# 24 warming matmuls where 14 stood, and a later place on ScalarE for the decay factors of group 0

## The chip, the cores and the metric

One core of a Trainium2 chip runs the whole program. The metric is device microseconds of one execution; the time of a kernel is the median of its runs. Five engines work beside each other, each in its own order: TensorE (PE, with its weight loads PEld), VectorE (DVE), ScalarE (ACT), GpSimd (POOL) and SyncE (SP), which issues most transfers.

## The reference

A decoder block on 256 tokens of 1024 channels, all in float32. The normalized input goes through one wide projection. Its columns feed a state-space mixer (8 groups of 4 heads, a causal convolution, a scan in chunks of 128 tokens), an attention of 16 heads, and gates. Both branches are projected, merged, projected once more and added to the input; a gated feed-forward part with a convolution and a last norm follow.

```python
hn = rmsnorm(x, norm1_w)
proj = hn @ w_in
z, xbc_raw, dt_raw, q, k, v, g_raw = jnp.split(proj, IN_OFFSETS, axis=-1)
y_ssd = ssd_mixer(z, xbc_raw, dt_raw, ssd_conv_w, ssd_conv_b, ssd_dt_bias, ssd_a_log, ssd_d, ssd_norm_w)
...
y_att = moba_attention(q, k, v.reshape(b, s, ATT_N_HEADS, ATT_HEAD_DIM))
...
merged = g_ssd * (y_ssd @ w_ssd_proj) + g_att * (y_att @ w_att_proj)
x = x + merged @ w_out
h2 = rmsnorm(x, norm2_w)
a, gb = jnp.split(h2 @ w_ffn_up, 2, axis=-1)
a = causal_dwconv(a, ffn_conv_w, ffn_conv_b)
return x + (jax.nn.silu(a) * gb) @ w_ffn_down
```

In the mixer the decay between two tokens of a chunk is an exponential of a difference of running sums, and it is multiplied by the product of C and B:

```python
L = jnp.exp(segsum(Adt))
CB = jnp.einsum('bclgn,bcsgn->bcgls', Cc, Bc)
y_diag = jnp.einsum('bcgls,bgrcls,bcsgrp->bclgrp', CB, L, Xc)
```

## The kernel before

The weights come in tiles of 1 MB, in the order of the list `seq`. Each tile (a unit here) is loaded into one of three `raw` buffers, and `split_unit` (L86) divides it in two halves. ScalarE casts each half to `hi` (L95), VectorE subtracts to get `lo` (L96). Four buffers of each hold two units. Activations are kept as such pairs too, so that a float32 product becomes three fast matmuls: hi by hi, hi by the lo of the other, lo by hi (L152 to L154 for a unit, 48 matmuls; L181 to L183 for the gates; L348 to L350 for v). `next_unit` returns unit i, issues loads up to i + 2 and writes the splits up to unit i + 1.

The head: `xtok` is loaded and its squares are summed; VectorE makes two diagonal matrices `dg` of the norm's factors (L266). Ahead of this TensorE multiplies a tile of ones by itself WARM times (L73), into a PSUM tile that nothing reads. Sixteen transposes (L271, eight for each half of the tokens) write x times `dg` into four PSUM tiles `xps`, two channel blocks in each. From these ScalarE casts the eight `hn` (L235), and VectorE makes their lo parts (L237). Then unit 0 can start on TensorE (`u_bc(0)`).

A group g of the mixer has the units bc, x, qk and then v, z or gate tiles. In group 0 the units are 0 bc, 1 x, 2 qk, 3 z, 4 and 5 the gates; group 1 has 6 bc, 7 x, 8 qk, 9 v, 10 z. The running sums of the decay go out to DRAM (`acsT_d`) and come back spread over all partitions (`acsB`), both by GpSimd's queue. `s_cb(g)` makes the product `pcb` on TensorE and its masked copy `cb` on VectorE; then ScalarE turns `acsB` into the decay factors `mx` with 13 activations (L376 to L379), and VectorE multiplies them by `cb` (L381). `s_y(g)` uses them in the product `py` (L403), which TensorE does behind unit x of the next group; the scores `s_ps` (L432) follow.

What sets the order: the tile scheduler orders the instructions of each engine by the program's order, priorities and its own estimate of times. TensorE has the program's order, once the head is over. `tc.issue_after(i)` keeps the instructions inside it behind instruction i on the engine; in `s_cb` they stand behind the tanh of z (`z_tanh`), in the last group behind the copy of q and k. Waits between engines are added by what is read and written.

Of the kernel before, what the change touches and what calls it, by code (L numbers as in the profile page):

```python
# [11 lines left out]
AF = mybir.ActivationFunctionType  # L12
# [10 lines left out]
NG = 8  # L23
# [10 lines left out]
C_DTB, C_AL = 304, 336  # L34
NPAR = 368

WARM = 14


def block_kernel(tc, xtok_d, par_d, nf_d, con_d, rope_d, wdt_d, win_d, wgate_d, bg_d, watt_d, wssd_d, wout_d, wup_d, wdn_d, out_d):  # L40
    nc = tc.nc
    st = ExitStack()
    pool = lambda name, bufs=1, **kw: st.enter_context(tc.tile_pool(name=name, bufs=bufs, **kw))
    with st:
# [26 lines left out]
        with tc.manual_schedule(engines=PE_ONLY):  # L71
            for _ in range(WARM):
                nc.tensor.matmul(warm[:, 0, 0:P], ones, ones, start=True, stop=True)  # L73
# [14 lines left out]
        def split_unit(raw, nk=KD):  # L88

            halves = []  # L90
            for k0 in range(0, nk, 4):
                n = min(4, nk - k0)
                hi = wpool.tile([P, 4, 256], F32R, tag="hi", bufs=4, name="hi")
                lo = wpool.tile([P, 4, 256], F32R, tag="lo", bufs=4, name="lo")
                nc.scalar.activation(hi[:, :n], raw[:, k0 : k0 + n], AF.Copy)  # L95
                split_unit.last = nc.vector.tensor_tensor(lo[:, :n], raw[:, k0 : k0 + n], hi[:, :n].bitcast(F32),  # L96
                                                          op=ALU.subtract)
                halves.append((hi, lo, n))
            return halves
# [21 lines left out]
        def next_unit():  # L121

            i = next_unit.i
            next_unit.i += 1
            load_to(i + 3)
            while len(units) < min(i + 2, len(seq)):
                n = len(units)
                units.append(split_unit(raws[n], seq[n][1]))
            return units[i]
# [3 lines left out]
        def mm_unit(ps, halves, act, first=True, last=True, k0=0, apart=False):  # L133


            tiles = [(hi, lo, kk) for hi, lo, n in halves for kk in range(n)]
            nk = len(tiles)
            km = [(k, m) for k in range(nk) for m in range(2)]
            if apart:
                km.sort(key=lambda x: x[1])  # L140
                ps = [p[:, 0, :] for p in ps]
            else:
                ps = [ps[:, m, :] for m in range(2)]
            with tc.manual_schedule(engines=PE_ONLY):
                for k, m in km:
                    hi, lo, kk = tiles[k]
                    xh, xl = act[k0 + k][:, 0, :], act[k0 + k][:, 1, :]
                    wh = hi[:, kk, m * P : m * P + P]
                    wl = lo[:, kk, m * P : m * P + P]
                    a = first and k == 0 and (m == 0 or apart)  # L150
                    z = last and k == nk - 1 and (m == 1 or apart)
                    nc.tensor.matmul(ps[m], wh, xh, start=a, stop=False)  # L152
                    nc.tensor.matmul(ps[m], wh, xl, start=False, stop=False)  # L153
                    nc.tensor.matmul(ps[m], wl, xh, start=False, stop=z)  # L154
# [30 lines left out]
        def mm_tile():  # L185
            return ps_mm.tile([P, 2, T], F32, tag="mm", bufs=3, name="mm")
# [108 lines left out]
        S = [dict() for _ in range(NG)]  # L295
# [4 lines left out]
        def u_bc(g):  # L300
            hv = next_unit()
            ps = mm_tile()
            mm_unit(ps, hv, hn)
            bc = S[g]["bc"] = ssp.tile([P, 2, T], F32, tag="bc", bufs=1, name="bc")
            conv_silu(bc, ps, (16 + g, 24 + g))

        def u_x(g):
            hv = next_unit()
            ps = mm_tile()
            mm_unit(ps, hv, hn)  # L310
            xs = S[g]["xs"] = ssp.tile([P, 2, T], F32, tag="xs", bufs=2, name="xs")
            conv_silu(xs, ps, (2 * g, 2 * g + 1))
# [50 lines left out]
        def s_cb(g):  # L363
            bc = S[g]["bc"]
            pcb = ps_s.tile([P, 4, P], F32, tag="ss", bufs=2, name="pcb")
            nc.tensor.matmul(flat(pcb[:, 0:2]), bc[:, 0, 0:P], bc[:, 1, :], start=True, stop=True)
            nc.tensor.matmul(pcb[:, 2], bc[:, 0, P:T], bc[:, 1, P:T], start=True, stop=True)
            cb = ssp.tile([P, 3, P], F32, tag="cb", bufs=1, name="cb")
            nc.vector.tensor_tensor(cb, pcb[:, 0:3], mmask, op=ALU.mult)
            acsB = S[g]["acsB"]  # L370
            mx = S[g]["mx"] = ssp.tile([P, 4, 3, P], F32, tag="mx", bufs=1, name="mx")
            with tc.issue_after(S[g]["qk_copy" if g == NG - 1 else "z_tanh"].ins):
                for r in range(4):
                    h = 4 * g + r
                    for c, b in ((0, 0), (1, 2)):
                        nc.scalar.activation(mx[:, r, b], acsB[:, r, c * P : c * P + P], AF.Relu, scale=-1.0,  # L376
                                             bias=acs[:, c, h : h + 1])
                    nc.scalar.activation(mx[:, r, 1], acsB[:, r, P:T], AF.Exp, bias=alm[:, h : h + 1])
                nc.scalar.activation(mx[:, :, 0:3:2], mx[:, :, 0:3:2], AF.Exp, scale=-1.0)  # L379
            m2 = mx.rearrange("p h b l -> p h (b l)")  # L380
            nc.vector.tensor_tensor(m2, m2, flat(cb)[:, None, :].to_broadcast([P, 4, 3 * P]), op=ALU.mult)  # L381

        def s_xt(g):
            xs = S[g]["xs"]
            pxt = ps_s.tile([P, 2, T], F32, tag="ss", bufs=2, name="pxt")
            for c in range(2):
                for m in range(2):
                    nc.tensor.transpose(pxt[:, c, m * P : m * P + P], xs[:, m, c * P : c * P + P], ident)
            xt = S[g]["xt"] = ssp.tile([P, 2, 4, 64], F32, tag="xt", bufs=1, name="xt")
            nc.vector.tensor_tensor(xt, pxt.rearrange("p c (h d) -> p c h d", h=4),  # L390
                                    dt[:, :, 4 * g : 4 * g + 4][:, :, :, None].to_broadcast([P, 2, 4, 64]), op=ALU.mult)
# [20 lines left out]
        def s_st(g):  # L412
            S[g]["ry"] = rms_stat([S[g]["sqy"][:, 0]], 1.0 / 256)
# [36 lines left out]
        def a_t(g):  # L450
            S[g]["pt"] = []
            for j in range(2):
                pt_ps = ps_s.tile([P, 4, P], F32, tag="at", bufs=2, name="pt_ps")
                for b in range(3):
                    nc.tensor.transpose(pt_ps[:, b], S[g]["pr"][j][:, b], ident)  # L455
                pt = atp.tile([P, 3, P], F32, tag="pt", bufs=2, name="pt")
                nc.scalar.activation(pt, pt_ps[:, 0:3], AF.Copy)
                S[g]["pt"].append(pt)
# [112 lines left out]
        def small_1(g):  # L571
            if 0 <= g - 1 < NG:
                s_y(g - 1)
                a_s(g - 1)
            if 0 <= g - 2:
                a_o(g - 2)
                if g < NG:
                    s_pb(g - 2)

        def small_2(g):  # L580
            if g < NG:
                s_cb(g)
                s_xt(g)
            if 0 <= g - 1:
                s_st(g - 1)
                a_t(g - 1)
            if g == NG:
                s_pb(g - 2)

        for g in range(NG):  # L590
            if g:
                u_bc(g)
                u_x(g)
                small_1(g)
                load_acs(g)
            u_qk(g)
            if g == 0:
                for c in range(2):
                    tc.keep_in_program_order(nc.gpsimd.dma_start(gates[:, c], bg_d.partition_broadcast(P)))
                u_z(g)  # L600
                turn_qk(g)
                dt_sums()
                gate = u_gate(0)
                next(gate)
                dt_turn()
                load_acs(0)
                next(gate)
                next(gate)
                small_2(g)
                next(gate)  # L610
            elif g == NG - 1:
                u_z(g)
                turn_qk(g)
                small_2(g)
                u_v(g)
            elif g % 2:
                u_v(g)
                turn_qk(g)
                u_z(g)
                small_2(g)  # L620
            else:
                u_z(g)
                turn_qk(g)
                gate = u_gate(g // 2)
                next(gate)
                next(gate)
                small_2(g)
                next(gate)
                next(gate)
# [187 lines left out]
        for h in range(2):  # L817
# [3 lines left out]
            hv, k0 = next_unit(), DOWN[-1][0]  # L821
# [125 lines left out]
```

## Time and profile before

| | us |
|---|---|
| median of 3 runs | 604.04 |
| lowest and highest run | 602.41, 607.84 |
| the profiled execution | 604.41 |
| its span, first to last instruction | 602.6 |

The profile is of one execution. A row of a timeline gives the start in us from the span's start, the duration in us (of several merged instructions together, with their number as x), engine, line, operation and tiles, and in brackets how long the engine was idle ahead of it and what ended that. A TensorE matmul lasts longer than the step to the next one, since they are pipelined. The granted clock is TensorE's, 1.00 being 2.4 GHz and 0.50 being 1.2 GHz.

### The profile page before, as it was taken

The page shows a single profiled execution, that of the slowest core. Times are in us where ns is not written, and L with a number is a line of the kernel's source. Part 1 is how long each engine was busy: PE and PEld are TensorE (multiplying, and loading weights), DVE is VectorE, ACT ScalarE, POOL GpSimd, SP SyncE. Part 2 cuts the span into 40 slices and gives each one's busy share as a digit, 9 for nine tenths or more (in the row PEclk, how much of TensorE's full clock was granted, in tenths as well). Part 3 has the DMA queues.
Part 4 walks back from the last instruction along what each step waited for, and adds up shares of the span by engine and source line. Part 5 has one row for each costly group of instructions (what it writes and reads, how often), then busy time and mean ns, then how long its engine had stood idle before and what let it go on. Part 6 is the DMA issues. An engine that isn't in the chain of part 4 may idle for free.

```text
span 602.6 us, 10067 instructions
## 1 busy us (share of the span) xinstructions
PE 589.6 (98%) x3886; PEld 528.6 (88%) x3886; DVE 459.8 (76%) x889; ACT 372.5 (62%) x675; POOL 17.9 (3%) x35
## 2 busy tenths in 40 slices
PE   7999999999999999999999999999999999999994
PEld 7899899999999999999998888889888888888883
DVE  3894989879798797978988446667888888884643
ACT  4654686866769567695686334456766666665432
POOL 0010000000000000010000000000000000000100
PEclk8999999999999999999999999999999999999997
DMA  8665646353363544645334855645456455464602
GB/s 314 238 230 239 234 156 212 136 218 140 145 232 139 193 141 148 241 145 176 140 129 157 291 187 185 206 152 201 154 197 204 155 200 205 123 228 150 239 34 70
DMA packets 17728, 109.73 MB, mean 182 GB/s; under 512 B 2177, under 2 KB 2561, under 8 KB 5649
## 3 DMA queue, kind: packets, MB, share of 16 engines
q1 hardware_dynamic: 15264, 100.42, 47.3%
q0 software_dynamic: 1984, 6.85, 3.1%
q10 hardware_dynamic: 432, 1.84, 0.8%
q8 instruction: 30, 0.49, 0.3%
q14 instruction: 18, 0.14, 0.1%
HBM read 107.49 MB, written 1.08 MB: 180 GB/s over the span
## 4 chain that ended last, share of the span: by engine, by line
PE 94%; DMA 3%; ACT 1%; issue 1%; DVE 1%; SPq 0%; ACTq 0%; DVEq 0%
PE up L164 12%; PE mm L152 10%; PE mm L154 10%; PE mm L153 10%; PE mm L181 10%; PE mm L182 10%; PE mm L183 10%; PE up L165 6%; PE py L403 2%; PE mm L348 1%; PE mm L350 1%; PE mm L349 1%; PE s_ps L432 1%; PE po L469 1%; DMA xtok<-in_xtok_dram 1%; PE pt_ps L455 1%
## 5 line engine op out<-in xcount | busy, mean ns | idle before, releaser
L96 DVE TENSOR_TENSOR lo<-raw,hi 128x1024 fp32r<-128x1024 f32 x186 | 227.1, 1226 | 83.6 <-ACT hi L95 82.8
L95 ACT ACTIVATE hi<-raw 128x1024 fp32r<-128x1024 f32 x186 | 195.0, 1056 | 142.1 <-PE mm L183 65.4
L152 PE MATMUL mm<-hn,hi 128*128 128x256 f32 x512 | 146.0, 285 | 0.4 <-ACT hi L95 0.4
L154 PE MATMUL mm<-hn,lo 128*128 128x256 f32 x512 | 144.9, 283 | 0.8 <-DVE lo L96 0.8
L153 PE MATMUL mm<-hn,hi 128*128 128x256 f32 x512 | 145.0, 283 | 0.4 <-DVE hn L237 0.4
L164 PE MATMUL up<-xw,hi 128*128 128x512 f32 x320 | 113.1, 399 | 0.0
L152 PEld LDWEIGHTS mm<-hn,hi 128*128 128x128 f32 x512 | 98.1, 192 | 1.5 <-ACT hi L95 0.9
L154 PEld LDWEIGHTS mm<-hn,lo 128*128 128x128 f32 x512 | 98.2, 192 | 1.0 <-DVE lo L96 1.0
L153 PEld LDWEIGHTS mm<-hn,hi 128*128 128x128 f32 x512 | 98.2, 192 | 0.9 <-DVE hn L237 0.8
L165 PE MATMUL up<-xw,lo 128*128 128x256 f32 x320 | 89.9, 281 | 0.0
L164 PEld LDWEIGHTS up<-xw,hi 128*128 128x128 f32 x320 | 60.1, 188 | 15.0
L165 PEld LDWEIGHTS up<-xw,lo 128*128 128x128 f32 x320 | 60.5, 189 | 0.0
L289 DVE SCALAR_TENSOR_TENSOR cacc<-mm,par,cacc 128x255 f32<-128x255 f32 (+2 forms) x96 | 44.5, 477 | 2.2 <-ACT cacc L285 1.4
L181 PE MATMUL mm<-hi,act 128*128 128x512 f32 (+1 forms) x92 | 34.9, 380 | 0.0
L182 PE MATMUL mm<-lo,act 128*128 128x512 f32 (+1 forms) x92 | 34.9, 380 | 0.0
L183 PE MATMUL mm<-hi,act 128*128 128x512 f32 (+1 forms) x92 | 34.9, 380 | 0.0
L181 PE MATMUL mm<-hi,hn 128*128 128x512 f32 x64 | 25.5, 398 | 0.0
L181 PE MATMUL mm<-hi,yn 128*128 128x512 f32 x64 | 25.2, 394 | 0.0
L376 ACT ACTIVATE mx<-acsB,acs 128x128 f32<-128x128 f32 x64 | 21.9, 391 | 5.1 <-DMA acsB<-acsT_d 5.1
L182 PE MATMUL mm<-lo,hn 128*128 128x512 f32 x64 | 25.0, 390 | 0.0
L183 PE MATMUL mm<-hi,hn 128*128 128x512 f32 x64 | 25.0, 390 | 0.0
L182 PE MATMUL mm<-lo,yn 128*128 128x512 f32 x64 | 24.9, 390 | 0.0
(196 smaller groups left out, 970.6 us busy)
## 6 DMA issues: line engine op xcount, KB each, us to landing
raw<-in_win_dram SPq DMA_DIRECT2D x35, 1024.0 KB, 4.8
raw<-in_wup_dram SPq DMA_DIRECT2D x22, 1024.0 KB, 4.8
raw<-in_wdn_dram SPq DMA_DIRECT2D x10, 1024.0 KB, 4.9
raw<-in_wgate_dram SPq DMA_DIRECT2D x8, 1024.0 KB, 5.0
raw<-in_wssd_dram SPq DMA_DIRECT2D x8, 1024.0 KB, 4.8
acsB<-acsT_d POOLq DMA_DIRECT2D x8, 512.0 KB, 4.5
raw<-in_watt_dram SPq DMA_DIRECT2D x4, 1024.0 KB, 5.0
raw<-in_wout_dram SPq DMA_DIRECT2D x4, 1024.0 KB, 5.1
```

What stands on the lines that cost most here:

```text
L95: nc.scalar.activation(hi[:, :n], raw[:, k0 : k0 + n], AF.Copy)
L96: split_unit.last = nc.vector.tensor_tensor(lo[:, :n], raw[:, k0 : k0 + n], hi[:, :n].bitcast(F32), op=ALU.subtract)
L152: nc.tensor.matmul(ps[m], wh, xh, start=a, stop=False)
L153: nc.tensor.matmul(ps[m], wh, xl, start=False, stop=False)
L154: nc.tensor.matmul(ps[m], wl, xh, start=False, stop=z)
L164: nc.tensor.matmul(ps[:, m].rearrange("p a b -> p (a b)"), wh, both, start=(k == 0), stop=False)
L165: nc.tensor.matmul(ps[:, m, 1], wl, act[k][:, 0, :], start=False, stop=(k == len(tiles) - 1))
L181: nc.tensor.matmul(o, xh, wh, start=(k == 0 if apart else k0 + k == 0), stop=False)
L182: nc.tensor.matmul(o, xh, wl, start=False, stop=False)
L183: nc.tensor.matmul(o, xl, wh, start=False, stop=(k0 + k == nk - 1))
L289: nc.vector.scalar_tensor_tensor(acc[:, s:], src[:, m, : T - s], w(m, 3 - s), acc[:, s:], op0=ALU.mult, op1=ALU.add)
L376: nc.scalar.activation(mx[:, r, b], acsB[:, r, c * P : c * P + P], AF.Relu, scale=-1.0, bias=acs[:, c, h : h + 1])
```

## The change

`WARM` is 24, not 14. `s_cb` is cut in two: `s_mx` is the part that makes `mx` and multiplies it, and takes the instruction behind which it stands. For groups 1 to 7 it is called where it stood, behind the same instruction. For group 0 it is called inside group 1, after `u_bc(1)`, behind the last hi split that has been written there, which is that of unit 7's second half.

```diff
--- before.py
+++ after.py
@@ -34,7 +34,7 @@
 C_DTB, C_AL = 304, 336
 NPAR = 368
 
-WARM = 14
+WARM = 24
 
 
 def block_kernel(tc, xtok_d, par_d, nf_d, con_d, rope_d, wdt_d, win_d, wgate_d, bg_d, watt_d, wssd_d, wout_d, wup_d, wdn_d, out_d):
@@ -92,7 +92,7 @@
                 n = min(4, nk - k0)
                 hi = wpool.tile([P, 4, 256], F32R, tag="hi", bufs=4, name="hi")
                 lo = wpool.tile([P, 4, 256], F32R, tag="lo", bufs=4, name="lo")
-                nc.scalar.activation(hi[:, :n], raw[:, k0 : k0 + n], AF.Copy)
+                split_unit.last_hi = nc.scalar.activation(hi[:, :n], raw[:, k0 : k0 + n], AF.Copy)
                 split_unit.last = nc.vector.tensor_tensor(lo[:, :n], raw[:, k0 : k0 + n], hi[:, :n].bitcast(F32),
                                                           op=ALU.subtract)
                 halves.append((hi, lo, n))
@@ -367,9 +367,12 @@
             nc.tensor.matmul(pcb[:, 2], bc[:, 0, P:T], bc[:, 1, P:T], start=True, stop=True)
             cb = ssp.tile([P, 3, P], F32, tag="cb", bufs=1, name="cb")
             nc.vector.tensor_tensor(cb, pcb[:, 0:3], mmask, op=ALU.mult)
-            acsB = S[g]["acsB"]
+            S[g]["cb"] = cb
+
+        def s_mx(g, behind):
+            acsB, cb = S[g]["acsB"], S[g]["cb"]
             mx = S[g]["mx"] = ssp.tile([P, 4, 3, P], F32, tag="mx", bufs=1, name="mx")
-            with tc.issue_after(S[g]["qk_copy" if g == NG - 1 else "z_tanh"].ins):
+            with tc.issue_after(behind.ins):
                 for r in range(4):
                     h = 4 * g + r
                     for c, b in ((0, 0), (1, 2)):
@@ -580,6 +583,8 @@
         def small_2(g):
             if g < NG:
                 s_cb(g)
+                if g:
+                    s_mx(g, S[g]["qk_copy" if g == NG - 1 else "z_tanh"])
                 s_xt(g)
             if 0 <= g - 1:
                 s_st(g - 1)
@@ -590,6 +595,8 @@
         for g in range(NG):
             if g:
                 u_bc(g)
+                if g == 1:
+                    s_mx(0, split_unit.last_hi)
                 u_x(g)
                 small_1(g)
                 load_acs(g)
```

TensorE at the very start, after the change: `warm` are the warming matmuls, `xps` the transposes, and the last two rows begin unit 0.

```order
L73 MATMUL warm<-ones 128x128 x21
L271 MATMUL xps<-dg,xtok 128x128 x7
L73 MATMUL warm<-ones 128x128
L271 MATMUL xps<-dg,xtok 128x128 x2
L73 MATMUL warm<-ones 128x128
L271 MATMUL xps<-dg,xtok 128x128
L73 MATMUL warm<-ones 128x128
L271 MATMUL xps<-dg,xtok 128x128 x6
L152 MATMUL mm<-hn,hi 128x256
L153 MATMUL mm<-hn,hi 128x256
```

Before, 14 warming matmuls stood there in a row and 16 transposes behind them; of the ten more, three now stand among the transposes.

ScalarE in the head, before the change: `hi` are the two halves of unit 0 and then of unit 1, `hn` the eight casts, `cacc` the convolution of unit 0.

```order
L95 ACTIVATE hi<-raw 128x1024
L235 ACTIVATE hn<-xps,par 128x256 x2
L95 ACTIVATE hi<-raw 128x1024
L235 ACTIVATE hn<-xps,par 128x256 x6
L95 ACTIVATE hi<-raw 128x1024 x2
L285 ACTIVATE cacc<-mm,par 128x256 x2
```

Here the second half's split stands between the second and the third cast.

And the same stretch of ScalarE after the change:

```order
L518 ACTIVATE nega<-par 128x32
L95 ACTIVATE hi<-raw 128x1024 x2
L235 ACTIVATE hn<-xps,par 128x256 x8
L95 ACTIVATE hi<-raw 128x1024 x2
L285 ACTIVATE cacc<-mm,par 128x256 x2
```

It moved ahead of all of them; on VectorE `lo` and the lo parts of `hn` moved alike.

ScalarE behind the decay factors of group 0, before the change: the first row is the last of their 13 activations, `gates` are the two gate tanhs, and the three `hi` are units 7b, 8a and 8b.

```order
L379 ACTIVATE mx<-mx 128x4x2x128
L566 ACTIVATE gates<-gates 128x512 x2
L95 ACTIVATE hi<-raw 128x1024 x3
L285 ACTIVATE cacc<-mm,par 128x256 x2
L95 ACTIVATE hi<-raw 128x1024
L292 ACTIVATE th<-cacc 128x256
```

After it the gate tanhs and the split of 7b stand ahead of the 13, and this follows them:

```order
L382 ACTIVATE mx<-mx 128x4x2x128
L285 ACTIVATE cacc<-mm,par 128x256 x2
L95 ACTIVATE hi<-raw 128x1024 x4
L292 ACTIVATE th<-cacc 128x256
L285 ACTIVATE cacc<-mm,par 128x256 x2
L292 ACTIVATE th<-cacc 128x256 x2
```

The four splits are units 8 and 9; the last of them moved ahead of the first tanh of unit 6's convolution.

VectorE in group 1, after the change, from the attention's maxima (ISA) to the split of unit 9's second half, the one `lo` here:

```order
L293 SCALAR_TENSOR_TENSOR xs<-th,cacc 128x256
L413 TENSOR_TENSOR zt<-zt 128x256
L444 TENSOR_SCALAR sm<-sm 128x2
L442 ISA pr,sm<-s_ps,con 128x128
L442 ISA sm 128x1
L442 ISA pr,sm<-s_ps,con 128x256
L442 ISA sm 128x1
L96 TENSOR_TENSOR lo<-raw,hi 128x1024
```

Before, this split stood earlier, between the last convolution step of unit 6 and the product `bc`, ahead of all of unit 7's convolution; behind the maxima came unit 10's.

## Rows read from the trace of the kernel before

**Rows 1.** The page's first part: busy time, share of the span, instructions.

```profile
PE 589.6 (98%) x3886; PEld 528.6 (88%) x3886; DVE 459.8 (76%) x889; ACT 372.5 (62%) x675; POOL 17.9 (3%) x35
```

**Rows 2.** TensorE's waits: us in total, times, longest.

```profile
PE xps L271 <- DVE dg L266: 2.2, 1, 2.2
PE warm L73 <- DVE ones L66: 1.1, 1, 1.1
PE mm L154 <- DVE lo L96: 0.8, 1, 0.8
PE mm L153 <- DVE hn L237: 0.4, 1, 0.4
PE mm L152 <- ACT hi L95: 0.4, 1, 0.4
```

**Rows 3.** TensorE's timeline in the head: start, duration, instructions, idle before.

```profile
1.05 5.64 PE L73 MATMUL warm<-ones 128*128 128x128 f32 x28 [1.05 <-DVE ones L66]
8.88 5.47 PE L271 MATMUL xps<-dg,xtok 128*128 128x128 f32 x32 [2.18 <-DVE dg L266]
...
16.54 0.38 PE L153 MATMUL mm<-hn,hi 128*128 128x256 f32 x1 [0.39 <-DVE hn L237]
...
20.71 0.28 PE L154 MATMUL mm<-hn,lo 128*128 128x256 f32 x1
```

**Rows 4.** TensorE's timeline in three short windows, x the records in each.

```profile
5.70 1.00 PE L73 MATMUL warm<-ones 128*128 128x128 f32 x7
...
10.67 1.70 PE L271 MATMUL xps<-dg,xtok 128*128 128x128 f32 x7
...
12.73 1.50 PE L271 MATMUL xps<-dg,xtok 128*128 128x128 f32 x12
```

**Rows 5.** Two windows: busy by engine, then granted clock, DMA share, GB/s.

```profile
10.00:11.00 1.00, 1.00 (x7) 1.00 (x6) 0.87 (x3) 0.51 (x1) 0.00 (x0) 0.50 1.04 389
13.00:14.00 1.00, 1.00 (x12) 1.00 (x11) 0.08 (x1) 0.95 (x3) 0.00 (x0) 1.00 0.99 418
```

**Rows 6.** ScalarE's timeline at the decay factors of group 0.

```profile
56.10 0.76 ACT L376 ACTIVATE mx<-acsB,acs 128x128 f32<-128x128 f32 x2 [5.09 <-DMA acsB<-acsT_d]
...
61.68 2.94 ACT L95 ACTIVATE hi<-raw 128x1024 fp32r<-128x1024 f32 x3
```

**Rows 7.** TensorE's timeline around unit 7b, the product and the scores.

```profile
62.11 0.28 PE L154 MATMUL mm<-hn,lo 128*128 128x256 f32 x1
...
66.86 1.52 PE L403 MATMUL py<-mx,xt 128*64 128x256 f32 x16
...
69.16 0.39 PE L152 MATMUL mm<-hn,hi 128*128 128x256 f32 x1
```

**Rows 8.** ScalarE's timeline in the head: the first two casts.

```profile
13.04 0.84 ACT L235 ACTIVATE hn<-xps,par 128x256 fp32r<-128x256 f32 x2 [2.54 <-PE xps L271]
```

**Rows 9.** The first weight tile's two loads: issue, and time to landing.

```profile
L85 SPq DMA_DIRECT2D raw<-in_win_dram x2: 432/432/432, 3.0 to 3.5; - x2
...
DMA to landing us min/median/max: 6.4/6.8/7.2
```

**Rows 10.** VectorE's timeline in the head.

```profile
10.54 1.23 DVE L96 TENSOR_TENSOR lo<-raw,hi 128x1024 fp32r<-128x1024 f32 x1
...
16.00 2.44 DVE L237 SCALAR_TENSOR_TENSOR hn<-xps,par,hn 128x256 fp32r<-128x256 f32 x6
```

**Rows 11.** VectorE's timeline from group 0 into group 1.

```profile
60.77 1.76 DVE L381 TENSOR_TENSOR mx<-mx,cb 128x1536 f32<-128x1536 f32 x1 [6.28 <-ACT mx L379]
62.76 3.50 DVE L96 TENSOR_TENSOR lo<-raw,hi 128x1024 fp32r<-128x1024 f32 x3 [0.23 <-ACT hi L95]
...
71.83 0.48 DVE L289 SCALAR_TENSOR_TENSOR cacc<-mm,par,cacc 128x255 f32<-128x255 f32 x1
72.23 0.47 DVE L407 SCALAR_TENSOR_TENSOR yg<-xs,par,py 128x256 f32<-128x256 f32 x1
...
77.74 1.22 DVE L96 TENSOR_TENSOR lo<-raw,hi 128x1024 fp32r<-128x1024 f32 x1
```
## The prediction

> **What bounds the kernel now.** I read the busy table first: TensorE is busy for 98% of the span [rows 1]. The reader is to see that another engine matters only where it makes TensorE wait. The list of TensorE's waits comes next [rows 2]. It has five entries, 4.8 us together, in a span of 602.6 us: 2.2 us ahead of the input transposes `xps` (for `dg`), 1.1 us for the first memset, and three smaller ones (0.8, 0.4, 0.4 us) in the projections. The change can win back only these, or work that TensorE does at half clock. So two stretches were read closely, 0 to 21 us and 50 to 78 us. I call unit n the n-th weight tile of `seq` (group 0 is units 0 to 5, group 1 begins with 6), and a and b its halves.
>
> In the head, 14 warming matmuls (28 records, two a matmul) run from 1.05 to 6.69 us, TensorE then idles for 2.2 us, and the 16 transposes (32 records) run from 8.88 to 14.35 us [rows 3]. The step from record to record tells the clock. Seven xps records from 10.67 us take 1.70 us; less the last one's own 0.42 us that is 1.28 / 6 = 0.213 us a step. Twelve from 12.73 us take 1.50 us, so (1.50 - 0.28) / 11 = 0.111 us [rows 4]. The granted clock beside them is 0.50 (1.2 GHz) and 1.00 (2.4 GHz) [rows 5]. The last seven warm records already went at (1.00 - 0.28) / 6 = 0.12 us [rows 4]: the clock had risen before 6 us, fell after the idle 2.2 us, and rose again within the transposes. All 32 at the fast step would take 31 x 0.111 + 0.28 = 3.7 us; they took 5.47, so (5.47 - 3.7) / 0.102 = 17 of them were slow. Then unit 0 starts, stops, and goes on at 16.54 us; its last matmul is at 20.71 us [rows 3].
>
> In the second stretch ScalarE stands still for 5.09 us in front of `mx` until `acsB` lands, and the hi split of unit 7b, queued behind it, starts only at 61.68 us [rows 6]. TensorE wants that half just after 62.11 us, and the product `py` that follows unit 7 starts at 66.86 us [rows 7].
>
> **The warm matmuls.** The new order puts 21 in front of the transposes and 3 among them. The seven more in front are 14 records. At the step of 0.12 us of the last warm ones they end at 6.69 + 14 x 0.12 = 8.4 us, ahead of `dg` (xps started at 8.88 us), so they delay nothing. At 0.213 us they would end at 9.7 us and delay by 0.8 us, the other end. I take the first: the same matmuls were fast by then. TensorE then idles 0.5 us, not 2.2. No row shows how the clock takes a gap of 0.5 us; 2.2 us behind some 1 us of fast work made it fall. I take it to stay at 2.4 GHz, because TensorE would have worked nearly all the time since the rise. The three inner ones cost 6 x 0.111 = 0.7 us. Then 32 + 6 = 38 records end at 8.88 + 37 x 0.111 + 0.28 = 13.3 us, not 14.35. The first PSUM tile is full after 24 records, at 8.88 + 23 x 0.111 + 0.28 = 11.7 us, where before ScalarE took it at 13.04 us [rows 8].
>
> **What the order of the splits does with it.** ScalarE now does both hi splits of unit 0 ahead of all eight `hn` casts, VectorE both lo splits ahead of all eight `hn` differences. Weight half 0b was issued at 3.5 us and landed 7.2 us later, at 10.7 us [rows 9]. So hi 0b (2.94 / 3 = 0.98 us a split [rows 6]) ends near 11.7 us, when the PSUM tile for the first `hn` is full anyway. VectorE's first lo ends at 10.54 + 1.23 = 11.77 us, the second at 13.0 us, and the differences follow at 2.44 / 6 = 0.41 us each [rows 10]: the first is done at 13.4 us, and each next one before TensorE, which stays on one `hn` for 6 x 0.12 = 0.72 us, asks for it. The second matmul of unit 0 thus starts at 13.4 us and the 48th 46 x 0.12 = 5.5 us later, at 19.0 us with a slow first record, where 20.71 us stood [rows 3]. **Term 1: 1.7 us gained.** With no wait for VectorE at all it would be 13.3 + 47 x 0.12 = 18.9 us, 1.8 us gained; the lower ends stand with the rivals. The next units don't hold it: TensorE waits for nothing else up to 62 us [rows 2], their splits follow its release of buffers, and the fourth load, which waits for lo 0b, goes out sooner.
>
> **The decay factors of group 0.** The 13 activations are the same; only their place moves, behind hi 7b and the two gate tanhs. They issue no transfer; the next `acsB` load on GpSimd's queue waits for them as it did. So hi 7b no longer stands behind the wait for `acsB`. Its buffer comes free when TensorE ends the gate unit, 72 matmuls x 0.12 = 8.6 us ahead of 62.2 us, near 53.6 us; hi and lo (0.98 and 1.23 us) are done by 56 us, over 6 us early (all in the times of before, from which term 1 goes off). Without the wait unit 7b takes 24 x 0.12 = 2.9 us from 62.23 us, and `py` starts at 65.2 us with 0.1 us for the new shape, where 66.86 us stood [rows 7]. **Term 2: 1.65 us gained.** That is more than the two named waits (0.4 and 0.8 us), since each restart has slow first records too.
>
> What is late next? On ScalarE the conv scalings of unit 6, the hi splits of units 8 and 9 and the conv tanhs now stand behind `mx`, which ends no later than before, since `acsB` sets its start. VectorE's product of `mx` still ends at 60.77 + 1.76 = 62.5 us [rows 11], 2.7 us before `py`. The tight place is lo 9b: VectorE's order now has it behind the softmax maxima. From 62.5 us on come three lo splits at 3.50 / 3 = 1.15 us and six conv and `bc` steps at 0.40 us (71.83 to 72.23), up to 68.3 us. Then come the operations that took 5.91 us from 71.83 to 77.74 us [rows 11], and two more at 0.40 us, so lo 9b runs from 75.0 to 76.3 us. TensorE asks for it at 65.2 + 2.3 (py and scores, 66.86 to 69.16 us [rows 7]) + 48 x 0.12 (unit 8) + 25 x 0.12 = 76.3 us. It just fits; I charge 0.05 us, and 1.0 us as the bound for an error in that chain.
>
> **Sum.** 1.7 + 1.65 - 0.05 = 3.3 us. The profiled execution took 604.41 us, so 601.1 us. It stands 0.37 us above the median of 604.04 us, so it is a usual run. Some 20 us later the orders of all engines are the same again, and TensorE waits for nothing there [rows 2]: nothing eats the lead and nothing adds to it.
>
> **The rivals.** (1) The clock falls in the gap all the same, and again 17 records are slow. The transposes end at 13.3 + 17 x 0.102 = 15.0 us, and unit 0, now without its stop, starts its last matmul at 20.6 us: 0.1 us gained, not 1.7, in all 602.7 us. For it: the clock did fall here. Against: the gap is a quarter as long.
>
> (2) The fall is an accident of this execution, and the clock mostly stays up in before. Its first PSUM tile would then be full after 20 records, at 8.88 + 19 x 0.111 + 0.28 = 11.3 us, 1.7 us ahead of 13.04, and the chain from there to the end of unit 0 would move by as much: nothing is left of term 1, and 602.8 us remain. For it: one run of before took 602.41 us, 2.0 us under the profiled one. Against: the median lies at the profiled time. The Trainium skill (TensorE: Matmul & The Clock Gate, "What's actually happening") says that the chip's watch over TensorE runs free of the kernel's start, so that the rise moves from run to run. By that rule before would have heads of both kinds; one trace can't tell.
>
> (3) Lo 9b is late by 1.0 us: 602.1 us.
>
> (4) Slower: weight half 0b lands late, and the `hn` casts, now behind its hi split on ScalarE, wait for it. The first difference is done 0.98 + 1.23 + 0.41 = 2.6 us after the landing. Term 1 is gone if it lands at 12.5 us and the whole gain at 14.1 us, not 10.7; landing 5 us late would cost 1.6 us, 606.0 us. For it: four other loads are under way then. Against: the load is issued when it was, with nothing new ahead of it.
>
> **How the numbers follow.** Forecast 0.52, rival 1 0.18, rival 2 0.13, rival 3 0.12, rival 4 0.05. The best case is 1.8 + 1.65 us, 601.0 us; the runs of before scatter by 1.6 us below their median, so the range begins at 599.3 us. A low clock together with a late lo 9b is 603.7 us, and with some scatter it ends at 604.2 us. A measurement of this kernel tells about 1%, 6 us, from no change. The terms can't reach that: within 1% has 0.92, faster 0.05 (a scatter like that of the run of 607.84 us in what is compared), slower 0.03 (the far end of rival 4).
>
> **What would show it.** In the trace of after: 42 warm records that end by 8.5 us; xps records 0.111 us apart from the first, at a granted clock of 1.00 around 10 us; hi 0b ahead of `hn`; unit 0's last matmul near 19.0 us; hi 7b near 52 us and no wait of TensorE for hi or lo near 60 us; `py` at 63.5 us; lo 9b within 0.3 us of its use. I am wrong if the step is 0.213 us, if TensorE waits ahead of unit 9b by more than 1 us, or if the lead at `py` is lost further on.

## The result, and the profile after

| | before | after |
|---|---|---|
| median, us | 604.67 (13 runs, 602.41 to 607.84) | 601.14 (13 runs, 600.55 to 601.97) |
| profiled execution, us | 604.41 | 601.73 |

The ratio is 0.9943, with a 95% interval of 0.9923 to 0.9963: 3.5 us gained, within 1%. The runs also lie closer together, 1.4 us where they were 5.4 us apart.

The page after begins with nearly the same busy time of TensorE (589.6 us before [rows 1]):

```profile
PE 589.4 (98%) x3906; PEld 529.3 (88%) x3906; DVE 459.9 (77%) x889; ACT 373.0 (62%) x675; POOL 18.0 (3%) x35
```

TensorE's waits in the trace of after (us in total, times, longest):

```profile
PE xps L271 <- DVE dg L266: 1.2, 1, 1.2
PE warm L73 <- DVE ones L66: 1.1, 1, 1.1
```

Of the five waits [rows 2] the three in the projections are gone, and the one for `dg` fell from 2.2 to 1.2 us. TensorE's timeline in the head, at the product `py` and at unit 9b:

```profile
1.06 7.22 PE L73 MATMUL warm<-ones 128*128 128x128 f32 x42 [1.06 <-DVE ones L66]
9.45 1.83 PE L271 MATMUL xps<-dg,xtok 128*128 128x128 f32 x14 [1.17 <-DVE dg L266]
...
12.46 1.50 PE L271 MATMUL xps<-dg,xtok 128*128 128x128 f32 x12
13.72 0.36 PE L152 MATMUL mm<-hn,hi 128*128 128x256 f32 x1
14.03 0.39 PE L153 MATMUL mm<-hn,hi 128*128 128x256 f32 x1
...
19.65 0.28 PE L154 MATMUL mm<-hn,lo 128*128 128x256 f32 x1
...
64.14 1.52 PE L406 MATMUL py<-mx,xt 128*64 128x256 f32 x16
...
75.30 0.28 PE L349 MATMUL mm<-lo,hn 128*128 128x256 f32 x1
```

Two windows of 1 us (busy, granted clock, DMA share, GB/s):

```profile
10.00:11.00 1.00, 1.00 (x11) 1.00 (x10) 0.86 (x5) 1.00 (x1) 0.00 (x0) 1.00 1.03 399
13.00:14.00 1.00, 1.00 (x10) 0.88 (x8) 1.00 (x3) 1.00 (x4) 0.00 (x0) 1.00 0.93 393
```

Around 10 us the clock was 0.50 [rows 5] and is 1.00: it did not fall in the gap between the warm records and the transposes. The step of the last twelve transposes is (1.50 - 0.28) / 11 = 0.111 us, as it was in the fast part before [rows 4], and (1.83 - 0.28) / 13 = 0.12 us holds from the first. The last matmul of unit 0 starts at 19.65 us, not 20.71 [rows 3], and `py` at 64.14 us, not 66.86 [rows 7].

ScalarE, in the head and at the decay factors:

```profile
8.04 0.63 ACT L261 ACTIVATE junk<-xtok 128x512 f32<-128x512 f32 x1 [1.55 <-DMA xtok<-in_xtok_dram]
...
11.26 1.06 ACT L95 ACTIVATE hi<-raw 128x1024 fp32r<-128x1024 f32 x1 [0.21 <-DMA raw<-in_win_dram]
12.44 3.03 ACT L235 ACTIVATE hn<-xps,par 128x256 fp32r<-128x256 f32 x8
...
52.79 1.06 ACT L95 ACTIVATE hi<-raw 128x1024 fp32r<-128x1024 f32 x1 [2.84 <-DVE gates L568]
...
54.95 0.70 ACT L379 ACTIVATE mx<-acsB,acs 128x128 f32<-128x128 f32 x2
```

VectorE, in the head and at the split of unit 9b:

```profile
11.09 2.49 DVE L96 TENSOR_TENSOR lo<-raw,hi 128x1024 fp32r<-128x1024 f32 x2
13.49 3.22 DVE L237 SCALAR_TENSOR_TENSOR hn<-xps,par,hn 128x256 fp32r<-128x256 f32 x8
...
73.71 1.22 DVE L96 TENSOR_TENSOR lo<-raw,hi 128x1024 fp32r<-128x1024 f32 x1
```

The square of the last part of `xtok` starts at 8.04 us here. In the trace of before the same instruction started at 7.47 us:

```profile
7.47 0.63 ACT L261 ACTIVATE junk<-xtok 128x512 f32<-128x512 f32 x1 [0.96 <-DMA xtok<-in_xtok_dram]
```

So the input landed 0.57 us later in this execution, and all that follows in the head is late by as much (the transposes start at 9.45, not 8.88 us). Less that, unit 0 gained 1.06 + 0.57 = 1.6 us. Hi 7b starts at 52.79 us ahead of `mx`, where it stood behind it at 61.68 us [rows 6], and nothing waits for it.

### The profile page after: what moved, and what is told of

The parts are those of the page before. It is cut to its first block, busy times and chain, and to the rows that moved or that the text cites. A ratio compares the mean times of both kernels' runs of the same rounds, so it can differ in the third digit from the quotient of the medians.

```text
span 600.0 us, 10104 instructions
## 1 busy us (share of the span) xinstructions
PE 589.4 (98%) x3906; PEld 529.3 (88%) x3906; DVE 459.9 (77%) x889; ACT 373.0 (62%) x675; POOL 18.0 (3%) x35
## 4 chain that ended last, share of the span: by engine, by line
PE 97%; DMA 1%; DVE 0%; ACT 0%; issue 0%; SPq 0%; DVEq 0%; ACTq 0%
PE up L164 13%; PE mm L152 11%; PE mm L153 11%; PE mm L154 11%; PE mm L181 11%; PE mm L182 11%; PE mm L183 11%; PE up L165 6%; PE py L406 2%; PE mm L348 1%; PE mm L349 1%; PE mm L350 1%; PE s_ps L435 1%; PE po L472 1%; DMA xtok<-in_xtok_dram 1%; PE pt_ps L458 1%
## 5 line engine op out<-in xcount | busy, mean ns | idle before, releaser
L289 DVE SCALAR_TENSOR_TENSOR cacc<-mm,par,cacc 128x253 f32<-128x253 f32 (+2 forms) x96 | 44.2, 477 | 2.5 <-ACT cacc L285 1.8
L181 PE MATMUL mm<-hi,yn 128*128 128x512 f32 x64 | 25.2, 394 | 0.0
L183 PE MATMUL mm<-hi,yn 128*128 128x512 f32 x64 | 24.9, 389 | 0.0
```

Source lines behind the costliest of these rows:

```text
L181: nc.tensor.matmul(o, xh, wh, start=(k == 0 if apart else k0 + k == 0), stop=False)
L183: nc.tensor.matmul(o, xl, wh, start=False, stop=(k0 + k == nk - 1))
L289: nc.vector.scalar_tensor_tensor(acc[:, s:], src[:, m, : T - s], w(m, 3 - s), acc[:, s:], op0=ALU.mult, op1=ALU.add)
```

## The experiments

The first four experiments share runs of the kernel before beside them (35 runs, median 604.01 us), the last four others (26 runs, 604.78 us). `py` less the last matmul of unit 0, both by their starts, is called the middle stretch here: 66.86 - 20.71 = 46.15 us in before, 64.14 - 19.65 = 44.49 us in after.

**The kernel before again.** No edit.

> The kernel before, unchanged, to see what its runs scatter with (602.4 to 607.8 us in 13 runs; after the change 600.6 to 602.0). Head theory: the clock fall in the gap ahead of the transposes comes in some runs only and costs 1.7 to 2.0 us, so runs near 602.5 us have a granted clock some 0.003 above those over 604 us (3.4 us at half clock is 0.0028 of the span). Landing theory: the scatter comes from the landing of acsB, for which ScalarE and behind it unit 7b wait; then the clock does not go with the time, and one more us of landing is one more us of time.

Median 604.80 us (12 runs, 602.51 to 605.96). The 12 runs part into two groups: five from 602.51 to 603.07 us, with mean granted clocks of 0.996 and 0.997, and seven from 604.62 to 605.96 us, with 0.990 to 0.995. The clock goes with the time. (A run's mean clock takes in the tail behind TensorE's last matmul, which runs at half clock: from 596.3 us to the end at 602.6 us in before, from 599.9 to 603.2 us in this experiment.) But the profiled execution, one of the seven (604.98 us, 0.994), had its fall in another place than the head. Its waits:

```profile
PE xps L271 <- DVE dg L266: 1.8, 1, 1.8
PE mm L152 <- ACT hi L95: 1.4, 1, 1.4
PE warm L73 <- DVE ones L66: 1.1, 1, 1.1
PE mm L154 <- DVE lo L96: 0.8, 1, 0.8
PE mm L153 <- DVE hn L237: 0.4, 1, 0.4
```

Its timeline, in the head and at `py`:

```profile
8.56 3.84 PE L271 MATMUL xps<-dg,xtok 128*128 128x128 f32 x32 [1.79 <-DVE dg L266]
...
18.76 0.28 PE L154 MATMUL mm<-hn,lo 128*128 128x256 f32 x1
...
67.37 1.52 PE L403 MATMUL py<-mx,xt 128*64 128x256 f32 x16
```

And its windows (us, TensorE busy, granted clock, DMA share, GB/s):

```profile
10.00:11.00 1.00, 1.00 (x11) 1.00 1.02 390
62.00:63.00 1.00, 0.32 (x2) 1.00 0.18 74
63.00:64.00 1.00, 0.93 (x7) 0.98 0.00 0
64.00:65.00 1.00, 1.00 (x7) 0.50 0.75 131
...
67.00:68.00 1.00, 1.00 (x11) 0.81 1.14 451
```

Here the head kept the full clock, with 14 warming matmuls: the transposes took 3.84 us, not 5.47, and unit 0 ended 1.95 us sooner than in the first trace (0.32 us of it since the input landed sooner). All of it was lost again at unit 7b. `acsB` came 1 us later behind TensorE, so the two waits, 0.4 and 0.8 us in before, were 1.4 and 0.8 us, and behind these the clock fell, in the middle of unit 7b, until past 67 us. The middle stretch is 67.37 - 18.76 = 48.61 us, 2.5 us longer than in the first trace: 1.0 us for the longer wait and 1.5 us for the clock. The better head did not make the wait longer. The store of the sums moved with it by the same 1.95 us (first row before, the two others this experiment), and it is the way through DRAM that took 1.0 us more:

```profile
45.93 0.52 POOL L533 DMA_DIRECT2D acsT_d<-acsT  x1 [6.61 <-ACT acsT L532]
...
43.98 0.52 POOL L533 DMA_DIRECT2D acsT_d<-acsT  x1 [6.61 <-ACT acsT L532]
...
55.13 0.76 ACT L376 ACTIVATE mx<-acsB,acs 128x128 f32<-128x128 f32 x2 [6.08 <-DMA acsB<-acsT_d]
```

So both theories of the scatter were half right: it is the clock that makes the steps of some 2 us, but it can fall in either place, and in this trace the landing of `acsB` decided one of them.

**Only the warming matmuls.** `WARM = 24` in the kernel before:

```diff
-WARM = 14
+WARM = 24
```

> Only the 24 warming matmuls, the decay factors where they stood. The head's order is that of after. Forecast's terms: 1.7 us gained (1.1 in an execution whose xtok lands 0.6 us late), so 602.9 us as a median, unit 0's last matmul near 19.0 us, and the wait of TensorE at unit 7b still there (0.4 and 0.8 us). Rival 2 (the fall was an accident): no gain in the median, under 0.5 us. Head theory of the scatter: runs within 1.5 us of each other. Landing theory: they still scatter by 4 to 5 us.

Median 603.07 us (12 runs, 602.58 to 605.08), ratio 0.9985 (0.9967 to 1.0003). The profiled execution kept the clock in the head, and the two waits at unit 7b stayed:

```profile
PE mm L154 <- DVE lo L96: 0.8, 1, 0.8
PE mm L152 <- ACT hi L95: 0.3, 1, 0.3
```

```profile
19.52 0.28 PE L154 MATMUL mm<-hn,lo 128*128 128x256 f32 x1
...
65.62 1.52 PE L403 MATMUL py<-mx,xt 128*64 128x256 f32 x16
```

The middle stretch is 46.10 us, as in before. The median moved by 0.9 us against the runs beside it and by 1.6 us against the 604.67 us of the 13 runs; the interval of the ratio takes in no change. What is clear is the spread: ten of the twelve runs lie within 1.0 us, as the head theory had it, and two above.

**Only the decay factors' place.** The change with the old number:

```diff
-WARM = 24
+WARM = 14
```

> Only the later place of the decay factors, 14 warming matmuls. Forecast's terms: 1.65 us gained, 603.0 us as a median, no wait of TensorE near 60 us, py 46.15 - 1.65 = 44.5 us behind the last matmul of unit 0. Rival 3: a wait at unit 9b eats up to 1 us of it. Head theory of the scatter: it stays at 2 us or more. Landing theory: it is gone, runs within 1.5 to 2 us, and the median gains more than 1.65 us, since landings later than the profiled one cost nothing any more.

Median 601.84 us (12 runs, 600.81 to 603.54), ratio 0.9962 (0.9943 to 0.9982): 2.2 us gained. The profiled execution:

```profile
8.17 5.46 PE L271 MATMUL xps<-dg,xtok 128*128 128x128 f32 x32 [1.97 <-DVE dg L266]
...
19.99 0.28 PE L154 MATMUL mm<-hn,lo 128*128 128x256 f32 x1
...
64.49 1.52 PE L406 MATMUL py<-mx,xt 128*64 128x256 f32 x16
...
76.31 0.39 PE L349 MATMUL mm<-lo,hn 128*128 128x256 f32 x1 [0.51 <-DVE lo L96]
```

The transposes took 5.46 us again: the clock fell in the head, as the clock of 0.992 of this run says. The middle stretch is 64.49 - 19.99 = 44.50 us, 1.65 us shorter than before, although `acsB` came back later here (ScalarE still waited 1.0 us for it). The last row is rival 3: TensorE waits 0.51 us for lo 9b. Six runs lie between 600.8 and 601.4 us and six between 602.3 and 603.5 us, so the landing theory's tight group did not come. Four of the upper six have mean clocks of 0.992 and 0.993, as the profiled one with its fall; two have 0.996 and 0.997, and what delayed these is not shown.

**The order of the splits with 14 warming matmuls.** The hi and lo splits of unit 0 written ahead of the `hn` in the kernel before, and the `hn` tied behind them:

```diff
+            units.append(split_unit(raws[0], seq[0][1]))
...
+            with tc.issue_after(split_unit.last_hi.ins):
+                for k in range(KD):
+                    nc.scalar.activation(hn[k][:, 0, :], xps[k // 2][:, k % 2], AF.Identity, scale=col(C_N1 + k))
+            with tc.issue_after(split_unit.last.ins):
```

> The kernel before with 14 warming matmuls, but with the head's order of after on ScalarE and VectorE: both hi and lo splits of unit 0 ahead of the eight hn. It tells the order from the clock. If the clock is what term 1 rests on: the fall stays, transposes end near 14.3 us, unit 0 runs without its stop from there, its last matmul at 14.4 + 47 x 0.12 = 20.0 us, 0.6 us gained of the 1.7. If the order alone makes term 1: last matmul near 19.0 us and 1.7 us gained.

Median 604.84 us (12 runs, 603.26 to 607.07), ratio 1.0008 (0.9985 to 1.0031): no gain. In the profiled execution the input landed 0.66 us later than in the first trace, TensorE idled 3.8 us, and the clock fell:

```profile
1.05 4.72 PE L73 MATMUL warm<-ones 128*128 128x128 f32 x28 [1.05 <-DVE ones L66]
9.54 5.47 PE L271 MATMUL xps<-dg,xtok 128*128 128x128 f32 x32 [3.77 <-DVE dg L266]
...
20.48 0.28 PE L154 MATMUL mm<-hn,lo 128*128 128x256 f32 x1
```

The transposes took the same 5.47 us. Unit 0 ended 0.23 us sooner, 0.9 us less the late landing. That is unit 0's stop, nearer to the 0.6 us that the clock's side expected than to the 1.7 us of the order's side. The middle stretch is 46.2 us as before, and in the median not even the 0.6 us can be seen.

**The changed kernel again.** No edit.

> The changed kernel unchanged, beside the three that follow. Median near 601.1 us, runs within 1.5 us of each other, one stretch of full clock from about 6 us to the end of TensorE's work. If the wait at unit 9b (rival 3) comes in some executions, the profile shows a few tenths of a us there.

Median 601.36 us (10 runs, 600.61 to 602.20), ratio 0.9954 (0.9933 to 0.9974). Its profile shows two waits, 1.1 us for the memset and 0.5 us for `dg`, no fall, and none at unit 9b.

**34 warming matmuls.** In the changed kernel:

```diff
-WARM = 24
+WARM = 34
```

> 34 warming matmuls: 21 still in front, 13 instead of 3 among the transposes. It prices the inner ones when nothing covers them. By the working of the prediction the 13 are 26 records x 0.111 = 2.9 us, the transposes end near 8.88 + 57 x 0.111 + 0.28 = 15.5 us and unit 0's last matmul starts at 21.1 us, some 2 us later than in after: 603.0 us. If the inner ones were free (they fill time in which TensorE waits for hn anyway): within 0.4 us of after.

Median 604.58 us (12 runs, 603.48 to 607.35), 3.2 us above the changed kernel beside it. TensorE's timeline, with the last of the inner warm matmuls, the end of unit 0, and the wait at unit 9b:

```profile
14.11 1.28 PE L73 MATMUL warm<-ones 128*128 128x128 f32 x10
...
20.85 0.28 PE L154 MATMUL mm<-hn,lo 128*128 128x256 f32 x1
...
77.85 0.39 PE L349 MATMUL mm<-lo,hn 128*128 128x256 f32 x1 [0.84 <-DVE lo L96]
```

Ten records of warm matmuls stand behind the last transposes, and unit 0 starts its last matmul at 20.85 us (19.21 us in the changed kernel's second profile). That is 1.6 us; counted from the first transpose (8.72 and 9.01 us) it is 1.9 us, the 2 us that were expected. What was not expected are two waits more: 0.84 us for lo 9b and 0.4 us in the sums of the decay. Together they are 2.8 us of the 3.0 us between the spans (602.5 and 599.5 us).

**21 warming matmuls and the same order.** The changed kernel with `WARM = 21` and the order of the fourth experiment.

> 21 warming matmuls, all in front, none among the transposes, and the order of hi, lo and hn written out as in after. It asks whether the three inner ones cost. My working: the transposes end 0.7 us sooner, but unit 0's second matmul waits for lo 0b and the first hn difference, 2.6 us behind the landing of half 0b, so the median is within 0.3 us of after. Rival: they cost their 0.7 us, and the median falls to 600.5 us.

Median 601.14 us (10 runs, 600.76 to 601.67), 0.2 us from the changed kernel beside it, which is not to be told from none. The three inner warm matmuls cost nothing, because unit 0 waits anyway:

```profile
9.34 3.84 PE L271 MATMUL xps<-dg,xtok 128*128 128x128 f32 x32 [1.74 <-DVE dg L266]
...
13.93 0.39 PE L153 MATMUL mm<-hn,hi 128*128 128x256 f32 x1 [0.64 <-DVE hn L280]
```

The transposes are one row of 3.84 us, 0.7 us shorter than the stretch from first to last in after (9.45 to 13.96 us); and TensorE stands 0.64 us in front of the second matmul for the first `hn` difference.

**21 warming matmuls alone.**

```diff
-WARM = 24
+WARM = 21
```

> The change with 21 warming matmuls. No inner ones, and the scheduler then puts six hn casts and differences ahead of the second half's splits. Unit 0 no longer waits for the landing of half 0b: it starts as the transposes end, near 12.6 us, and its last matmul starts near 18.3 us, 0.6 to 0.7 us ahead of after: 600.5 us. Rival: the k-tiles 4 to 7 then stop for lo 0b, which stands behind six differences (done near 15.8 us, wanted near 15.4 us), and eat 0.4 us of it: 600.9 us.

Median 600.73 us (7 runs, 600.30 to 603.69), 0.4 us below the seventh and 0.6 us below the fifth; six of the seven runs lie at or under 601.28 us. Its waits and its timeline:

```profile
PE xps L271 <- DVE dg L266: 1.7, 1, 1.7
PE warm L73 <- DVE ones L66: 1.1, 1, 1.1
```

```profile
9.40 3.84 PE L271 MATMUL xps<-dg,xtok 128*128 128x128 f32 x32 [1.71 <-DVE dg L266]
...
19.11 0.28 PE L154 MATMUL mm<-hn,lo 128*128 128x256 f32 x1
...
63.60 1.52 PE L406 MATMUL py<-mx,xt 128*64 128x256 f32 x16
```

Unit 0 no longer waits, and its last matmul starts 9.71 us behind the first transpose, where it took 19.65 - 9.45 = 10.20 us in after: 0.5 us, near the 0.6 to 0.7 us expected. This is the best version found and under both kernels by its median; but 0.4 to 0.6 us is less than these runs can part from the change as it is.

## Why the prediction was right

**The sum.** 601.1 us was forecast and 601.14 us measured, but against a median of before of 604.67 us in the end, so the gain was 3.5 us, not 3.3. Between the two profiled executions it was 2.7 us. That the forecast is met to 0.04 us is luck; that it is met within some tenths of a us is not.

**Term 1, 1.7 us.** In the two traces it is 1.06 us, and 1.6 us less the later landing of `xtok`. Its mechanism was right: 42 warm records end at 8.28 us, the clock stays up in a gap of 1.2 us, the transposes run at the full clock, both splits of half b stand ahead of `hn`, and the second matmul of unit 0 is what the order sets (the seventh experiment shows the wait). It starts at 14.03 us, 4.6 us behind the first transpose (4.5 us in the prediction). The gap was 1.2 us and not 0.5, since the warm step fell to 0.11 us and `dg` came later. What the inner ones cost was put at 0.7 us of TensorE's time and, rightly, at next to nothing for unit 0; the seventh experiment shows it, and the sixth shows the price of ten more that nothing covers. But the term is not gained in every run. The head of the first experiment, with 14 warming matmuls and the old order, kept the clock and took 18.76 - 8.56 = 10.20 us from the first transpose to the last matmul of unit 0, as long as the head of after. So the term is the clock's fall and not the order of the splits, and by this trace an execution of before without the fall has nothing to gain there.

**Term 2, 1.65 us.** The middle stretch is 1.66 us shorter in after, and 1.65 us in the third experiment. But the 1.65 us belong to one landing of `acsB`. In the first experiment's trace the same wait cost 2.5 us more than in the trace of before, with a fall of the clock in it. The prediction took this wait as a constant of the kernel. In the medians moving `mx` brought 2.2 us (third experiment) and the warming matmuls alone 0.9 us (second, both against the same runs); the intervals of both take in the 1.65 and the 1.7 us of the terms. Both together brought 3.4 us in the fifth.

**"So it is a usual run".** This step was half right. The runs of before are of two kinds. In the ten traces, the six without a fall of the clock ahead of the tail have a mean of 0.995 to 0.997, the four with one 0.992 to 0.994. Sorted by that mark, after the fact, 35 of the 73 runs of before whose clock is on record (the first experiment and the runs beside all eight) had no fall, with a median of 602.74 us, and 38 had one or more, with 605.1 us. Single runs don't part cleanly (one at 0.995 took 606.30 us). Against the runs without a fall beside them, the warming matmuls alone gain nothing (eleven such runs, 603.02 against 602.78 us), the place of `mx` alone gains 1.5 us (eight, 601.25 us) and both gain 1.3 us (all ten of the fifth, 601.36 against 602.62 us). So, by this sorting, term 2 comes in all runs, and what is gained beyond it only against those of before that lose the clock, in the head or at unit 7b, about half of them. The median of before lay among these by its time, as the profiled run did, so the sum held.

**Rival 1** (the clock falls all the same) did not happen in any trace with 42 warm records in front: the gaps were at most 1.7 us, and the clock held in each. With 28 records in front it held over 1.8 us once and fell behind 2.0 us, so the traces don't tell whether the number of warm records does anything beyond filling the gap: no run had 42 of them and a gap of 2 us.

**Rival 2** (the fall is an accident) was right in that before has heads of both kinds. The same 28 warm records took 5.64 us in before, 5.70 us in the first experiment, 5.15 us in the third and 4.72 us in the fourth, so the fast step began at other points. The Trainium skill (TensorE: Matmul & The Clock Gate, "What's actually happening") has the rise move from run to run, and these traces agree. The rival's price was wrong: its 602.8 us take term 2 off an execution that has the fall. A before that mostly keeps the clock would itself stand near 602.7 us, as the 35 runs do, and after still near 601.1 us. It also left out that unit 7b can lose the clock where the head kept it.

**Rival 3** (lo 9b) is real, but not in after: lo 9b is done at 73.71 + 1.22 = 74.93 us and wanted at 75.30, so 0.4 us were spare where the prediction had none. It costs 0.5 us in the third experiment and 0.84 us in the sixth. There `acsB` landed later (ScalarE waited 1.0 and 1.4 us for it, and not at all in after), and with it the product of `mx` and VectorE's work behind it. So a late landing still costs something in the changed kernel.

**Rival 4** (half 0b lands late) was not seen: its hi split starts at 11.26 us in after, 0.6 us later than worked out, in an execution in which everything landed 0.6 us later. No run delayed that load on purpose.

## What to carry to other kernels

Warming matmuls are worth what they keep, not what they warm: fill the gap up to the first real matmul until the clock holds over what is left of it (up to 1.7 us here), and stop there, since each further one that the scheduler puts among the real ones costs its time as soon as nothing covers it. An in-order engine should not wait for a round trip through DRAM in front of work that the bounding engine needs soon; put the waiting block behind that work. A wait that is long enough to let the clock fall costs more than its own length (1.5 us more in the first experiment). And where such a fall comes in half of the runs, one profiled execution does not tell what a change is worth in the median: sort the runs by their clock first.

## What the runs showed of the hardware that was not expected

The granted clock fell behind idle stretches of TensorE of 2.0 us (third experiment), 2.2 us (before) and 3.8 us (fourth) in the head, and behind two waits of 1.4 and 0.8 us, close together, in the first experiment; it held behind 0.5 to 1.8 us there, and behind the two waits of 0.4 and 0.8 us. The clock's record says 1.00 for the first warm records too, though their step was 0.213 us, that of half the clock: it begins only with the first change.

The way of the decay sums through DRAM took 10.2 us from the issue of the store to the first `mx` in before (45.93 to 56.10 us), and 11.2 us in the first experiment (43.98 to 55.13 us), with the same transfers. In the seven traces in which ScalarE waited for it, it took 10.1 to 11.4 us.
